# Skip factors loaded as one row, and the compressed keys and values computed in two column halves of the array, in a decoder trunk block on one core

## The chip, the cores and the metric

The kernel runs on one core of one Trainium2 chip, as a single launch. The metric is the device time of a run in microseconds, as the median of several runs. The profile is of one execution, and its span is a little shorter than that execution's time.

## What is computed

One layer of a decoder trunk on `x` of shape (1, 512, 1024), fp32: 512 tokens (S), width 1024 (D).

```
h = RMSNorm(x);  u = h @ W_in            # one projection, its columns split among the heads below
y_A = DSA(u_A) @ W_br_A                  # an index picks 128 keys a query, then softmax attention
y_B = NSA(u_B) @ W_br_B                  # compressed keys, selected blocks, window; gated sum
y_C = SSD(u_C) @ W_br_C                  # Mamba-2: causal conv, chunked scan, gated RMSNorm
x = x + (sig(g_A) y_A + sig(g_B) y_B + sig(g_C) y_C) @ W_out
x = x + relu(RMSNorm(x) @ W_1)^2 @ W_2
```

Two small parts of it matter here:

```
# NSA: 31 blocks of 32 tokens, 16 apart, become one compressed key and one compressed value each
blocks = a[:, win_idx] + pos                       # a = keys (v = 0) or values (v = 1), 2 head groups
k_cmp  = rms_norm(einsum('bnlgd,lde->bnge', blocks, w[0]), gain);  v_cmp = einsum(..., w[1])
# SSD: a skip term with one factor for each of the 32 heads
y = y_diag + y_off + xs * d_skip
```

## The kernel before, in words

All big matrices are multiplied in three float32r products: both operands are split into a high part (a rounding copy, on ScalarE) and a low part (the difference, on VectorE or GpSimd), and high x high, high x low and low x high are summed in PSUM (`mm3`, lines 458 to 460). Weights come in blocks of 128 x 1024 by a stream (`WS`): a load on SP's queue into one of three raw buffers (line 154), a split into `whi` (line 173) and `wlo` (line 175) in one of six buffers each. The next load into a raw buffer waits until its split is done, and the next split until a block has been used up.

At the start the input is loaded in four blocks of 128 tokens (t = 0 to 3) and normalised; PE transposes each block in two halves (line 427) into PSUM tiles `pT`, of which there are two, and ScalarE and VectorE write the transposed block as `hTh` (line 437) and `hTl` (line 438). A `pT` tile is free again when both have read it. Beside it runs the first projection, `c0` (DSA's key and value, the index's operands, dt), token block after token block: 24 matmuls of 456 columns for each.

Two generators are interleaved in program order by estimated PE time. The filler makes the projections, in the order c0, nkv, dq, z, x, nq and then the gates and the branch products. The main one makes the DSA index with its top-k steps on VectorE (lines 899 and 900), DSA's attention, the SSD scan and NSA's attention. Which instruction follows which on an engine is then set by the scheduler of the Tile framework, which has a time model of its own and some written-out priorities; on each engine the instructions run in that order.

Small constants (gains, convolution weights, dt's bias and so on) are loaded in `const_load`, called in the filler when block t = 1 of c0 is done, all on SP's queue. Some come as rows and are transposed on PE in `const_cols`, called at block t = 1 of nkv, and copied from PSUM by VectorE (lines 355 to 359). The skip factors are wanted as `dcol`, 128 partitions x 16, one column for each 128 channels, with one head in partitions 0 to 63 and another in 64 to 127, halved. The scaling of the convolved channels in `conv` (line 860) reads it.

In `cmp_prep` the compressed keys and values are made on PE, for each of the two in 16 fp32 matmuls, one for each pair of positions of a block (line 659). The stationary operand is `xc`, 128 x 64 (two positions x 64 dims by 2 groups x 32 blocks), the streamed one 64 columns of the weights. An fp32 matmul shows as two passes in the trace, with a weight load each.

Of the kernel before, what the change touches and what calls it, by code (L numbers as in the profile page):

```python
# [9 lines left out]
AF = mybir.ActivationFunctionType  # L10
ALU = mybir.AluOpType
# [30 lines left out]
def build_kernel(ctx, tc, A, out):  # L42
    nc = tc.nc
    pe, act, dve, pool = nc.tensor, nc.scalar, nc.vector, nc.gpsimd
    done = set()

    def dram(ap, off, dims):
        return bass.AP(tensor=ap.tensor, offset=ap.offset + off, ap=dims)

    def bc(ap, shape):  # L50
        return ap.to_broadcast(shape)

    def f(ap):
        return ap.bitcast(F32)
# [37 lines left out]
    def ps(tag, shape, dt=F32, bufs=2):  # L92
        if tag == XT[0]:
            XT[1] += 1
            if XT[1] % 3 == 0:
                tag = "pF"
        return psp.tile(shape, dt, tag=tag, name=tag, bufs=PSB[tag])
# [27 lines left out]
    p = ps("pF", [128, 512])  # L125
# [159 lines left out]
    for q in range(3):  # L285
        m = 0
# [32 lines left out]
    dcol = cp.tile([128, 16], F32, name="dcol")  # L319
    CL = {}  # L320

    def const_load():
        def put(t, ap, n, rows=None):
            nc.sync.dma_start(t, dram(ap, 0, [[n, rows] if rows else [0, 128], [1, n]]))

        def rows(name, ap, r, n=128):
            CL[name] = early.tile([r, n], F32, name=name)
            put(CL[name], ap, n, r)

        def wide(name, ap, n):  # L330
            CL[name] = early.tile([128, n], F32, name=name)
            put(CL[name], ap, n)
        wide("gq_d", A["dsa_q_norm"], 64)
        wide("gk_d", A["dsa_k_norm"], 64)
        wide("gq_n", A["nsa_q_norm"], 64)
        wide("gk_n", A["nsa_k_norm"], 192)
        rows("rows1", A["ssd_conv_w"], 96)
        rows("rows2", A["ssd_conv_b"], 24)
        rows("rows3", A["ssd_norm_g"], 16)
        rows("posr", A["nsa_cmp_pos"], 64, 64)  # L340
        put(dtb, A["ssd_dt_bias"], 32)
        put(alog, A["ssd_a_log"], 32)
        for e in range(2):
            nc.sync.dma_start(dcol[64 * e:64 * e + 64], dram(A["ssd_d"], e, [[0, 64], [2, 16]]))
        dve.tensor_scalar(dcol, dcol, 0.5, None, op0=ALU.mult)
        dve.tensor_tensor(g_dsa, CL["gq_d"], CL["gk_d"], op=ALU.mult)
        dve.tensor_tensor(g_nsa, CL["gk_n"].rearrange("p (a b) -> p a b", b=64), bc(CL["gq_n"][:, None, :], [128, 3, 64]), op=ALU.mult)

    def const_cols():
        p = ps("pT", [128, 512])  # L350
        pe.transpose(p[:, 0:96], CL["rows1"], ident[:96, :96])
        pe.transpose(p[:, 96:120], CL["rows2"], ident[:24, :24])
        pe.transpose(p[:64, 120:184], CL["posr"], ident[:64, :64])
        pe.transpose(p[:, 184:200], CL["rows3"], ident[:16, :16])
        dve.tensor_copy(convc, p[:, 0:120])
        dve.tensor_copy(gcol, p[:, 184:200])
        pv_ = p[:64, 120:184].rearrange("p (v a l) -> p v a l", v=2, l=2)
        dve.tensor_copy(pos2[0:64], pv_[:, :, :, 0])
        dve.tensor_copy(pos2[64:128], pv_[:, :, :, 1])
# [29 lines left out]
    for t in range(NB):  # L389
        with tc.high_priority(offset=0 if t else HP):  # L390
# [5 lines left out]
            else:  # L396
# [3 lines left out]
                for k0 in range(0, KT, 4):  # L400
                    p = ps("pT", [128, 4, 128])
# [11 lines left out]
            else:  # L413
# [4 lines left out]
                for c in (0, 512):  # L418
                    p = ps("sc", [128, 512])
# [3 lines left out]
            for k0 in range(0, KT, 4):  # L423
                if t:
                    p = ps("pT", [128, 4, 128])
# [19 lines left out]
    for i, b in enumerate((2, 3)):  # L445
        for half in range(2):
            cur = 2 * b + half
            r = slice(64 * half, 64 * half + 64)
# [82 lines left out]
    def rms_rows(pl, src, rows, nb, scale, bias):  # L531
        sqt = pl.tile([128, NB, 64], F32, name="sqk")
        dve.tensor_tensor(sqt[:rows, :nb], src, src, op=ALU.mult)
        st = pl.tile([128, NB], F32, name="stk", bufs=2)
        dve.tensor_reduce(st[:rows, :nb], sqt[:rows, :nb], AX.X, ALU.add)
        dve.tensor_scalar(st[:rows, :nb], st[:rows, :nb], scale, bias, op0=ALU.mult, op1=ALU.add)
        rt = pl.tile([128, NB], F32, name="rtk", bufs=2)
        pool.tensor_tensor(rt[:rows, :nb], st[:rows, :nb], mhalf[:rows, :nb], op=ALU.pow)
        return rt
# [96 lines left out]
    def cmp_prep(u1, e1):  # L636

        for v in range(2):
            xc = e1.tile([128, 16, 2, 32], F32, name="xc", bufs=1)
            wh = []  # L640
            for i in range(2):
                w_ = e1.tile([128, 8, 64], F32, name="cmpw", tag="cw", bufs=2)
                nc.sync.dma_start(w_, dram(A["nsa_cmp_w"], v * 131072 + i * 65536, [[64, 128], [8192, 8], [1, 64]]))
                wh.append(w_)
            pool.memset(xc[:, :, :, 31:32], 0.0)
            p = ps("pT", [128, S])
            for t in range(NB):
                pe.transpose(p[:, t * 128:t * 128 + 128], u1[:, t, v * 128:v * 128 + 128], ident)
            yield 440
            for g in range(2):  # L650
                for half in range(2):
                    r = slice(64 * half, 64 * half + 64)
                    base = p[64 * g:64 * g + 64, half:half + 1]
                    win = bass.AP(tensor=base.tensor, offset=base.offset, ap=[base.ap[0], [2, 16], [16, 31]])
                    dve.tensor_tensor(xc[r, :, g, :31], win, bc(pos2[r, v, :, None], [64, 16, 31]), op=ALU.add)
            yield 440
            pc = ps("pT", [128, 512])
            for a in range(16):
                pe.matmul(pc[:64, :64], xc[:, a].rearrange("p g n -> p (g n)"), wh[a // 8][:, a % 8], start=a == 0, stop=a == 15)
            if v == 0:  # L660
                kx = e1.tile([64, 64], F32, name="kx")
                dve.tensor_copy(kx, pc[:64, :64])
                yield 1800
                rt = rms_rows(e1, kx[:, None, :], 64, 1, 1.0 / 64, EPS)
                dve.scalar_tensor_tensor(kx, kx, rt[:64, 0:1], g_nsa[:64, 0, :], op0=ALU.mult, op1=ALU.mult)
                kcs = e1.tile([64, 2, 2, 64], F32R, name="kcs")
                kxb = bc(kx[:, None, :], [64, 2, 64])
                act.activation(kcs[:, 0], kxb, AF.Copy)
                dve.tensor_tensor(kcs[:, 1], kxb, f(kcs[:, 0]), op=ALU.subtract)
                for i in range(2):  # L670
                    pk = ps("pT", [128, 64], F32R)
                    pe.transpose(pk, kcs[:, i].rearrange("p a b -> p (a b)"), identr[:64, :64])
                    act.activation(kc[:, :, i], f(pk).rearrange("p (g n) -> p g n", g=2), AF.Copy)
                yield 600
            else:
                vx = e1.tile([64, 64], F32, name="vx")
                dve.tensor_copy(vx, pc[:64, :64])
                yield 1800
                sel = e1.tile([64, 2, 4, 32], F32, name="sel")
                dve.tensor_copy(sel, bc(ident[:64, 0:64].rearrange("p (g n) -> p g n", g=2)[:, :, None, :], [64, 2, 4, 32]))  # L680
                zero = e1.tile([128, 256], F32, name="zero")
                pool.memset(zero, 0.0)
                vzf = vz.rearrange("p a b c d -> p (a b c d)")
                for z in range(2):
                    act.activation(vzf[:, 256 * z:256 * z + 256], zero, AF.Copy)
                for g in range(2):
                    pk = ps("pT", [128, 64])
                    pe.matmul(pk, sel[:, g].rearrange("p a b -> p (a b)"), vx, start=True, stop=True)
                    for h in range(4):
                        r = slice(32 * h, 32 * h + 32)  # L690
                        act.activation(vz[r, g, h % 2, 0], pk[r], AF.Copy)
                        dve.tensor_tensor(vz[r, g, h % 2, 1], pk[r], f(vz[r, g, h % 2, 0]), op=ALU.subtract)
                    yield 300

    def filler():
# [40 lines left out]
        def do_nkv():  # L736
# [27 lines left out]
            def rest():  # L764
                for g in range(2):
                    tr = make_k(u2[:, :, 64 * g:64 * g + 64], g_nsa[:, 2, :], K[f"w{g}"])
                    yield 0
                    tr()
                    yield 0
                dve.tensor_scalar(gate, gate, 0.5, 0.5, op0=ALU.mult, op1=ALU.add)  # L770
                yield from cmp_prep(u1, e1)
                pclose("e1")
                pclose("early")
                done.add("nkv")
# [1030 lines left out]
    while True:  # L1805
        with tc.high_priority(offset=HI[0]):
            r = next(mg, None)
# [42 lines left out]
```

## Time and profile before

| What | us |
|---|---|
| median of 3 runs | 1374.2 (1374.09 to 1375.94) |
| the profiled execution: time, span | 1373.8, 1372.1 |
| PE busy | 1334.8 |
| VectorE (DVE) busy | 995.5 |
| ScalarE (ACT) busy | 727.6 |
| GpSimd (POOL) busy | 269.9 |

Lines of the profile name an engine, a line of the kernel and a tile: `PE pT L427` is the matmul of line 427 that writes `pT`. PEld is PE's weight load, SPq, ACTq and so on are the queues of an engine, and a load is named by its destination and source. An idle time is shown with what released it.

### The profile page before, as it was taken

Reading aid. Unit: us, or ns where it says so; the run is one execution under the profiler, and the core shown is the slowest. Engines: PE = TensorE matmul, PEld = TensorE weight load, DVE = VectorE, ACT = ScalarE, POOL = GpSimd, SP = SyncE. Lnnn points to the kernel's source line nnn. Section 1 sums busy time; section 2 is a strip of 40 time slices with the busy share of each in tenths; the row PEclk is TensorE's granted clock in tenths of the full one; section 3 lists DMA queues with packets and bytes.
Section 4 is the critical chain, followed back from the end, with each engine's and each line's share of the span. In section 5 each row is a group of like instructions: output and inputs, shape, how many; then the busy total and the mean of one; then the engine's idle time right before and its main releaser. Section 6 shows DMA issues by size and latency. Waiting matters only on the chain.

```text
span 1372.1 us, 19609 instructions
## 1 busy us (share of the span) xinstructions
PE 1334.8 (97%) x6827; PEld 1113.0 (81%) x6827; DVE 995.5 (73%) x1970; ACT 727.6 (53%) x1393; POOL 269.9 (20%) x242
## 2 busy tenths in 40 slices
PE   6899999999999999999999999999999999999998
PEld 5788888888887777888888888787879888888887
DVE  4469997788987767457768798979745666767741
ACT  4355525577777776347666655656334344444430
POOL 2135201111005667600000021113001201102000
PEclk8899999999999999999999999999999999999999
DMA  4335655555559999564336453434535655746531
GB/s 141 99 116 144 163 161 150 152 135 155 143 145 327 304 276 318 181 176 119 112 113 180 119 152 117 147 119 144 193 94 168 129 165 125 182 114 130 151 123 50
DMA packets 253713, 213.73 MB, mean 156 GB/s; under 512 B 17817, under 2 KB 205101, under 8 KB 253614
## 3 DMA queue, kind: packets, MB, share of 16 engines
q1 hardware_dynamic: 237644, 188.88, 45.9%
q0 software_dynamic: 15232, 20.98, 8.1%
q10 hardware_dynamic: 738, 2.63, 0.5%
q8 instruction: 54, 0.88, 0.3%
q14 instruction: 45, 0.37, 0.1%
HBM read 171.74 MB, written 40.70 MB: 155 GB/s over the span
## 4 chain that ended last, share of the span: by engine, by line
PE 82%; DMA 7%; DVE 6%; ACT 2%; issue 2%; POOL 1%; SPq 0%; DVEq 0%; ACTq 0%; POOLq 0%
PE pj L458 19%; PE pj L459 19%; PE pj L460 19%; PE sc L460 3%; PE sc L459 3%; PE sc L458 3%; PE pT L983 2%; DMA dcol<-in_ssd_d_dram 2%; PE sc L924 2%; PE sc L923 2%; PE pv L995 2%; PE pv L996 1%; PE sc L1311 1%; DMA yr<-yc_d 1%; DMA E<-ac_d 1%
## 5 line engine op out<-in xcount | busy, mean ns | idle before, releaser
L173 ACT ACTIVATE whi<-wraw 128x1024 fp32r<-128x1024 f32 (+2 forms) x190 | 198.3, 1047 | 256.9 <-PE pj L459 136.8
L175 DVE TENSOR_TENSOR wlo<-wraw,whi 128x1024 fp32r<-128x1024 f32 (+1 forms) x176 | 223.3, 1273 | 99.6 <-ACT whi L173 99.2
L458 PE MATMUL pj<-hTh,whi 128*128 128x512 f32 x512 | 203.7, 398 | 2.3 <-DVE cacc L852 2.0
L460 PE MATMUL pj<-hTh,wlo 128*128 128x512 f32 x512 | 202.6, 396 | 0.0
L459 PE MATMUL pj<-hTl,whi 128*128 128x512 f32 x512 | 202.4, 395 | 0.0
L932 ACT ACTIVATE p<-p,nb,rs 128x256 f32<-128x256 f32 (+3 forms) x160 | 107.8, 676 | 34.2 <-DVE nb L930 34.1
L458 PEld LDWEIGHTS pj<-hTh,whi 128*128 128x128 f32 x512 | 96.7, 189 | 21.8 <-ACT eab L1340 2.2
L460 PEld LDWEIGHTS pj<-hTh,wlo 128*128 128x128 f32 x512 | 96.7, 189 | 18.9 <-issue 0.2
L459 PEld LDWEIGHTS pj<-hTl,whi 128*128 128x128 f32 x512 | 96.5, 189 | 18.5 <-issue 0.2
L458 PE MATMUL pj<-yh,whi 128*128 128x512 f32 (+1 forms) x288 | 106.1, 373 | 4.1 <-ACT yh L828 3.1
L459 PE MATMUL pj<-yl,whi 128*128 128x512 f32 (+1 forms) x288 | 107.2, 372 | 0.1
L460 PE MATMUL pj<-yh,wlo 128*128 128x512 f32 (+1 forms) x288 | 106.1, 368 | 0.0
L459 PE MATMUL pj<-h2l,whi 128*128 128x512 f32 (+1 forms) x256 | 96.3, 376 | 0.0
L460 PE MATMUL pj<-h2h,wlo 128*128 128x512 f32 (+1 forms) x256 | 96.2, 376 | 0.0
L458 PE MATMUL pj<-h2h,whi 128*128 128x512 f32 (+1 forms) x256 | 96.1, 376 | 0.0
L458 PE MATMUL pj<-whi,hTh 128*128 128x512 f32 (+2 forms) x208 | 81.4, 391 | 3.2 <-DVE v_s L560 2.2
L460 PE MATMUL pj<-whi,hTl 128*128 128x512 f32 (+2 forms) x208 | 80.6, 388 | 0.0
L459 PE MATMUL pj<-wlo,hTh 128*128 128x512 f32 (+2 forms) x208 | 80.1, 385 | 0.0
L1042 POOL DMA_DIRECT2D qu<-q_d x32 | 23.6, 738 | 272.4 <-PE sc L924 165.5
L987 ACT ACTIVATE pth<-pT 128x512 fp32r<-128x512 f32 x95 | 54.9, 593 | 32.1 <-PE pT L983 28.6
L458 PE MATMUL sc<-whi,fh 128*128 128x512 f32 x168 | 65.4, 389 | 0.0
L459 PE MATMUL sc<-wlo,fh 128*128 128x512 f32 x168 | 65.4, 389 | 0.0
(408 smaller groups left out, 3159.5 us busy)
## 6 DMA issues: line engine op xcount, KB each, us to landing
wraw<-in_w_in_dram SPq DMA_DIRECT2D x84, 512.0 KB, 3.9
wraw<-in_w_ff_dram SPq DMA_DIRECT2D x58, 512.0 KB, 4.1
qd<-in_w_ff_dram POOLq DMA_DIRECT2D x18, 512.0 KB, 5.8
gld<-g_d SPq DMA_DIRECT2D x35, 256.0 KB, 2.7
q_d<-qev SPq DMA_DIRECT2D x64, 128.0 KB, 3.3
qu<-q_d POOLq DMA_DIRECT2D x32, 256.0 KB, 3.6
E<-ac_d SPq DMA_DIRECT2D x16, 512.0 KB, 6.7
xz<-xzt_d SPq DMA_DIRECT2D x16, 512.0 KB, 5.2
```

The lines of the kernel that those rows point to most:

```text
L173: act.activation(hi[:, :m], r[:, :m], AF.Copy)
L175: (pool if i in LOWP else dve).tensor_tensor(lo[:, :m], r[:, :m], f(hi[:, :m]), op=ALU.subtract)
L458: pe.matmul(o, lh, rh, start=first, stop=False)
L459: pe.matmul(o, lh, rl, start=False, stop=False)
L460: pe.matmul(o, ll, rh, start=False, stop=last)
L923: pe.matmul(s_[:, h % w, :n], u.q[h], kh[:, :n], start=True, stop=False)
L924: pe.matmul(s_[:, h % w, :n], u.q[h], kl[:, :n], start=False, stop=True)
L932: act.activation(u.p[h][:, :n], u.p[h][:, :n], AF.Exp, bias=u.nb[:, h:h + 1], scale=rs8[:, u.b, u.h0 + h:u.h0 + h + 1], accum_out=u.sm[:, ...
L983: pe.transpose(pt[:, h], u.p[h][:, kb * 128:kb * 128 + 128], ident)
L987: act.activation(ph, ptf, AF.Copy)
L995: pe.matmul(o, vk, ph0, start=st, stop=False)
L1042: pool.dma_start(q.rearrange("p (i a) c -> p i (a c)", i=2), src)
```

## The change

The skip factors are no longer loaded into `dcol` by two loads of single numbers from the 32 factors. One load brings all 32 as a row, the same for all 128 partitions, into a tile `dsk` (`wide` is the helper for that, used for other constants too). Two VectorE instructions in `const_cols`, one for each half of the partitions, then write every second factor, halved, to `dcol`. The one VectorE instruction that halved `dcol` in `const_load` goes.

The 16 products of `cmp_prep` alternate between the lower 64 and the upper 64 PSUM partitions of the output, that is, between two column halves of the array. So each half has 8 of the 16 positions summed up. ScalarE copies the upper half to SBUF, and VectorE adds the lower half to it, where VectorE copied the one sum before.

```diff
@@ const_load
         put(dtb, A["ssd_dt_bias"], 32)
         put(alog, A["ssd_a_log"], 32)
-        for e in range(2):
-            nc.sync.dma_start(dcol[64 * e:64 * e + 64], dram(A["ssd_d"], e, [[0, 64], [2, 16]]))
-        dve.tensor_scalar(dcol, dcol, 0.5, None, op0=ALU.mult)
+        wide("dsk", A["ssd_d"], 32)
@@ const_cols
         dve.tensor_copy(convc, p[:, 0:120])
         dve.tensor_copy(gcol, p[:, 184:200])
+        for e in range(2):
+            r = slice(64 * e, 64 * e + 64)
+            dve.tensor_scalar(dcol[r], CL["dsk"].rearrange("p (m e) -> p m e", e=2)[r, :, e], 0.5, None, op0=ALU.mult)
@@ cmp_prep
             for a in range(16):
-                pe.matmul(pc[:64, :64], xc[:, a].rearrange("p g n -> p (g n)"), wh[a // 8][:, a % 8], start=a == 0, stop=a == 15)
+                o_ = 64 * (a % 2)
+                pe.matmul(pc[o_:o_ + 64, :64], xc[:, a].rearrange("p g n -> p (g n)"), wh[a // 8][:, a % 8], start=a < 2, stop=a > 13)
             if v == 0:
                 kx = e1.tile([64, 64], F32, name="kx")
-                dve.tensor_copy(kx, pc[:64, :64])
+                act.activation(kx, pc[64:128, :64], AF.Copy)
+                dve.tensor_tensor(kx, kx, pc[:64, :64], op=ALU.add)
...
                 vx = e1.tile([64, 64], F32, name="vx")
-                dve.tensor_copy(vx, pc[:64, :64])
+                act.activation(vx, pc[64:128, :64], AF.Copy)
+                dve.tensor_tensor(vx, vx, pc[:64, :64], op=ALU.add)
```

## The prediction

> **What bounds the kernel now.** I read the page first: the busy shares, then the chain that ended last.
>
> ```profile
> span 1372.1 us, 19609 instructions
> PE 1334.8 (97%) x6827; PEld 1113.0 (81%) x6827; DVE 995.5 (73%) x1970; ACT 727.6 (53%) x1393; POOL 269.9 (20%) x242
> PE pj L458 19%; PE pj L459 19%; PE pj L460 19%; PE sc L460 3%; PE sc L459 3%; PE sc L458 3%; PE pT L983 2%; DMA dcol<-in_ssd_d_dram 2%; PE sc L924 2%; PE sc L923 2%; PE pv L995 2%; PE pv L996 1%; PE sc L1311 1%; DMA yr<-yc_d 1%; DMA E<-ac_d 1%
> ```
>
> PE is the bound: it is idle in only 1372.1 - 1334.8 = 37.3 us, so a gain must shorten PE's work or fill an idle stretch. The odd item of the chain is a load: dcol, which holds 16 numbers a partition. Next, the waits of the first 60 us (total, times, longest).
>
> ```profile
> ACT hTh L437 <- PE pT L427: 25.7, 4, 16.6
> DVE dcol L345 <- DMA dcol<-in_ssd_d_dram: 18.0, 1, 18.0
> PE pT L427 <- DVE hTl L438: 15.4, 1, 15.4
> ```
>
> So VectorE stands 18.0 us at the halving of dcol, and PE has one wait of 15.4 us, 41% of all its idle time. The chain of the same window (start, us, what) shows how they hang together.
>
> ```profile
> 17.60 22.15 DMA dcol<-in_ssd_d_dram
> ...
> 39.85 0.17 DVE dcol L345
> 40.02 0.60 DVE hTl L438
> ...
> 40.67 1.12 PE pT L427 x4
> 41.79 0.38 PE sc L460
> ...
> 45.97 0.38 PE sc L459
> 46.35 0.70 PE pT L427 x4
> 47.05 0.21 PE sc L460
> ...
> 53.87 0.21 PE sc L460
> 54.08 0.23 PE pj L458
> ```
>
> The second load lands at 39.75; L345 runs; the hTl subtraction queued behind it frees a pT bank; PE can then transpose token block 3. PE restarts slowly: its 12 matmuls from 41.79 to 46.35 take 0.38 us each, the 34 from 47.05 to 54.08 take 7.03 / 34 = 0.207. At 54.08 the first projection (c0) is over and nkv begins. The timeline says what was ready meanwhile.
>
> ```profile
> 20.79 1.10 DVE L175 TENSOR_TENSOR wlo<-wraw,whi 128x912 fp32r<-128x912 f32 x1
> 22.36 1.08 ACT L437 ACTIVATE hTh<-pT 128x512 fp32r<-128x512 f32 x2 [2.77 <-PE pT L427]
> 23.34 1.06 ACT L173 ACTIVATE whi<-wraw 128x1024 fp32r<-128x1024 f32 x1
> 24.89 0.36 PE L459 MATMUL sc<-wlo,hTh 128*128 128x456 f32 x1
> 39.93 1.28 DVE L438 TENSOR_TENSOR hTl<-pT,hTh 128x512 fp32r<-128x512 f32 x2
> ```
>
> VectorE's last work ends at 21.89, both hTh halves are there at 23.44, and the two hTl subtractions need 1.28: without the wait they end near 24.7, before PE runs dry at 24.89 + 0.36 = 25.25.
>
> **The change, part by part.** First the loads: KB each and median us to landing; then an issue on SP.
>
> ```profile
> dcol<-in_ssd_d_dram SPq DMA_DIRECT2D x2, 4.0 KB, 12.4
> alog<-in_ssd_a_log_dram SPq DMA_DIRECT2D x1, 16.0 KB, 2.9
> wraw<-in_w_in_dram SPq DMA_DIRECT2D x84, 512.0 KB, 3.9
> 21.92 7.21 SPq L154 DMA_DIRECT2D wraw<-in_w_in_dram  x1
> ```
>
> Two loads of 64 x 16 single numbers, every second one, become one load of a contiguous row of 32 on 128 partitions. That is exactly the shape of alog, issued just ahead of dcol, which landed in 2.9 us with four times the bytes. The small loads also held SP: the weight load issued at 21.92 took 7.21 us to issue. I take 2.9 us for the new load. It stays at its place in SP's queue, as one issue instead of two, for which I count nothing.
>
> The halving leaves VectorE's early queue and goes, as two instructions, behind the copies of the column constants. There, and in the work after it, the trace has:
>
> ```profile
> 79.27 0.18 DVE L359 COPY pos<-pT 64x32 f32<-64x32 f32 x1
> 79.48 1.92 DVE L894 SCALAR_TENSOR_TENSOR mask<-irelu,iwt,caus 128x256 f32<-128x256 f32 x1
> 81.91 2.60 DVE L533 TENSOR_TENSOR sqk<-u 128x256 f32<-128x256 f32 x1
> 85.69 0.41 PE pj L458
> ```
>
> The load is long there by then. But VectorE is late at this place: the chain runs through sqk to PE at 85.69, so two instructions like L359's, 2 x 0.17, can push PE back. I count +0.3; the lower end is 0 (PE's wait there has other causes beside), the upper 0.4. The first reader of dcol, the scaling in conv (L860), comes at 290 us.
>
> The stall goes whole, by this working. PE's way from 25.25 to 54.08 is 28.83 us. Unstalled it is 2 x 0.70 for the transposes, 12 x 0.207 and the 7.03 of the rest: 1.40 + 2.48 + 7.03 = 10.91. The gain is 28.83 - 10.91 = 17.92: 15.42 idle, 0.42 on the first transposes and 2.08 of slow matmuls. What is late next? nkv would begin near 36.2. Its first weight block was split on ScalarE at 23.34, and the next two, issued by 21.92, need 3.9 us once nothing blocks them: there by about 26. The fourth is issued when VectorE has split the first (near 26) and lands near 30; nkv uses blocks 0 and 1 for two token blocks first, 4 x 6 x 0.23 = 5.5 us, so wants it at 41. So the cover is over 10 us. Everything after hangs on PE and moves forward with it.
>
> The products of the compressed keys and values: the chain's rows for the 16 fp32 matmuls (32 passes) of each, with the row after, and those of a product already written to alternating column halves (sc<-E,xt) and a full-width one beside it.
>
> ```profile
> 125.91 2.01 PE pT L659 x32
> 127.92 0.43 PE pj L460
> ...
> 155.80 2.01 PE pT L659 x32
> ...
> 469.86 0.89 PE sc L1311 x8
> ...
> 471.61 1.03 PE sc L1311 x16
> ```
>
> A pass of L659 takes 2.01 / 32 = 63 ns with 64 columns streamed. The full-width L1311 takes 0.89 / 8 = 111 ns for 128 columns, and the alternating one 1.03 / 16 = 64 ns, also for 128. So alternating halves do run side by side, but a pass comes no faster than 63 to 64 ns, whether 64 or 128 columns wide. L659 is at that floor already. I take no gain; the ends are -2.0 (both products halved) and +0.4, since the matmul behind L659 takes 0.43 instead of 0.23 and that 0.2 could come once more for each product. The Trainium skill, "TensorEngine Tiling (Array Packing)", section Theoretical Speedup, gives a factor up to 2 where a free dimension is at most 64; by that the products would take 2.0 us less. Its page "TensorE: Matmul & The Clock Gate" (Wait — 56ns, not 53.3ns?) knows an issue cost of about 62 ns per matmul with hardware decode off, by which nothing is gained; L659's 63 ns agrees. "Key Properties" of the tiling page speaks against the change, as changing the mode drains the engine; L659's 0.43 may be such a cost, already paid.
>
> Reading the result out: instead of one VectorE copy from PSUM, ScalarE copies the upper half and VectorE adds.
>
> ```profile
> L662 DVE COPY kx<-pT x1: 205/205/205, 128.9 to 128.9; 64x64 f32<-64x64 f32 x1
> L692 DVE TENSOR_TENSOR vz<-pT,vz x8: 194/220/231, 165.2 to 169.5; 32x64 fp32r<-32x64 f32 x8
> L673 ACT ACTIVATE kc<-pT x2: 224/224/224, 142.3 to 143.6; 128x64 fp32r<-128x64 f32 x2
> 128.61 0.60 ACT L893 ACTIVATE irelu<-sc 128x512 f32<-128x512 f32 x1 [1.42 <-PE sc L891]
> ACT whi L173 <- issue: 8.1, 3, 4.4
> ```
>
> VectorE's part is equal within 0.02 us. ScalarE's 0.22 fits for kx: it idles 1.42 us before 128.61, while the products end at 127.92 and VectorE comes at 128.9. The added wait is VectorE's on that copy; behind it stand the top-k steps of the index, which set the masks. If ScalarE is held by a weight split waiting for its buffer, VectorE waits too: at most 4.4 us, the longest of ScalarE's such waits in 100 to 180 us, for each product. The nearest rows say zero for kx; I take +0.2 for both, ends 0 and 8.8.
>
> Sum: -17.9 + 0.3 + 0 + 0.2 = -17.4. The profiled execution took 1373.8, its span and 1.7 around; 1373.8 - 17.4 = 1356.4. The median of the runs shown is 0.4 above it: **1356.8 us**.
>
> **The rivals.**
> The halves do overlap, against the floor I read: 2.0 less, 1354.8. For it speaks the 64 ns of a twice as wide pass; against it that the narrow one is no faster.
>
> PE's slow restart stays, or a weight block comes late by as much: only the idle 15.4 is won, so 1373.8 - 15.4 + 0.5 + 0.4 = 1359.3. For it: PE has just done transposes when it comes there; against it: the matmuls ahead of them ran at 0.21.
>
> ScalarE's copy holds VectorE, the rival on the other side: 8.8 at most by the row above, minus the 0.2 counted, gives 1365.4. It decides against the change only if VectorE waits over 17.4 us more in the two places and all of it reaches PE; the transposes that need kx follow 13 us after it, and no wait of ScalarE in that window comes near half of it.
>
> The change doesn't do what it says: the new load is as slow, or another load in the same stretch holds VectorE as long: 1374.2. alog's 2.9 us speaks against it.
>
> Last, a scheduler with a time model orders every engine's queue, so an edit can reorder work far from it. From PE's later waits (the largest group is 3.1 us in three) I estimate up to 5 us either way, 1352 to 1362 around the forecast.
>
> ```profile
> PE pj L458 <- ACT yh L828: 3.1, 3, 1.2
> ```
>
> **How the numbers follow.** Forecast 0.60, halves overlap 0.14, slow restart or late block 0.10, copy holds VectorE 0.06 (0.02 of it past break-even), no effect 0.03, reordering past its 5 us in the good or bad direction 0.07. The range holds the first three with the reordering, 0.84 less what falls off its edges: 1352 to 1363. About 0.2% is what a measurement of this kernel can tell from no change. Faster by more: all but 0.02 past break-even and 0.03 without effect, 0.95; within: 0.03; slower: 0.02.
>
> **What would show it.** Right: no wait of VectorE for a load of ssd_d, no PE idle of microseconds between 20 and 40 us, matmuls of the last two token blocks of c0 at 0.21 throughout, nkv's first matmul near 36, and the products still near 2.0 us each. Wrong in part: the products near 1.0; 0.38 us matmuls after 25; VectorE idle on kx or vx. The forecast as a whole fails if another wait for a load stands in VectorE's queue before 40 us, or if PE waits for nkv's weights near 36.

## The result, and the profile after

| | median, us | lowest to highest |
|---|---|---|
| before | 1374.2 | 1372.68 to 1375.94 |
| changed | 1364.12 | 1362.66 to 1369.46 |

The ratio is 0.9936, with an interval of 0.9910 to 0.9961. The change makes the kernel faster by 10.1 us, where 17.4 were forecast. The five runs of the changed kernel lie in two groups, three near 1363 and two near 1369; the profile is of the slowest, so it is read here for places and not for its end.

The span and the busy times of the profile after:

```profile
span 1367.7 us, 19598 instructions
PE 1335.8 (98%) x6827; PEld 1110.2 (81%) x6827; DVE 993.2 (73%) x1971; ACT 729.4 (53%) x1395; POOL 277.8 (20%) x242
```

PE's idle time fell from 37.3 to 1367.7 - 1335.8 = 31.9 us only, although a wait of 15.4 was to go. Did that wait go? The timeline around the old stall, VectorE first, then PE (start, us, engine, line, operation):

```profile
20.73 0.35 DVE L357 TENSOR_SCALAR dcol<-dsk 64x16 f32<-64x16 f32 x2 [0.18 <-DMA dsk<-in_ssd_d_dram]
21.79 1.29 DVE L439 TENSOR_TENSOR hTl<-pT,hTh 128x512 fp32r<-128x512 f32 x2 [0.70 <-ACT hTh L438]
...
23.66 0.37 PE L460 MATMUL sc<-wlo,hTh 128*128 128x456 f32 x1
23.86 0.60 PE L428 MATMUL pT<-ident,x 128*128 128x128 f32 x4
24.22 0.45 PE L461 MATMUL sc<-whi,hTl 128*128 128x456 f32 x1
...
34.05 0.37 PE L461 MATMUL sc<-whi,hTl 128*128 128x456 f32 x1
34.26 0.39 PE L459 MATMUL pj<-whi,hTh 128*128 128x512 f32 x1
```

It did. VectorE waits 0.18 us for the row instead of 18.0 for the single numbers, the transposes (L428) follow the matmuls with no gap, and nkv begins at 34.26 where it began at 54.08: PE is 19.8 us ahead at this place. At the end the medians show 10.1: about half of the lead is given back. So the question is where, and by which part of the change.

### The profile page after: what moved, and what is told of

The parts are those of the page before. It is cut to its first block, busy times and chain, and to the rows that moved or that the text cites. A ratio compares the mean times of both kernels' runs of the same rounds, so it can differ in the third digit from the quotient of the medians.

```text
span 1367.7 us, 19598 instructions
## 1 busy us (share of the span) xinstructions
PE 1335.8 (98%) x6827; PEld 1110.2 (81%) x6827; DVE 993.2 (73%) x1971; ACT 729.4 (53%) x1395; POOL 277.8 (20%) x242
## 5 line engine op out<-in xcount | busy, mean ns | idle before, releaser
L936 ACT ACTIVATE p<-p,nb,rs 128x256 f32<-128x256 f32 (+3 forms) x160 | 107.8, 676 | 40.2 <-DVE nb L934 38.3
L459 PEld LDWEIGHTS pj<-yh,whi 128*128 128x128 f32 x288 | 53.9, 190 | 19.4 <-ACT yh L832 7.6
L992 DVE TENSOR_TENSOR ptl<-pT,pth 128x512 fp32r<-128x512 f32 x95 | 64.0, 680 | 3.2 <-ACT pth L991 3.0
```

Of the source, the lines that this page charges most:

```text
L459: pe.matmul(o, lh, rh, start=first, stop=False)
L936: act.activation(u.p[h][:, :n], u.p[h][:, :n], AF.Exp, bias=u.nb[:, h:h + 1], scale=rs8[:, u.b, u.h0 + h:u.h0 + h + 1], accum_out=u.sm[:, ...
L992: dve.tensor_tensor(pl, ptf, f(ph), op=ALU.subtract)
```

## The experiments

One comparison stands ahead of them, of instructions and not of times. The row load alone leaves the order of the instructions as before, but for dcol's own load and halving: PE's 6,827 weight loads stand in the same sequence in the traces of before and e1. As soon as the read-out of the products is edited, the scheduler puts more than a quarter of them at other places, far from the edit. Call these the old order (before) and the new order (after). Two theories follow. Theory 1: the stall is worth what was forecast, and the edit of products and read-out costs some 8 us, by the order that it brings. Theory 2, the rival: the work that starts earlier collides later with transfers and buffers, so the stall was worth only some 8 us, and the rest is neutral.

**The two parts alone, the products without the halves, and the change again.** The edits, in this sequence:

```
e1_row_only            the diff of const_load and const_cols alone
e2_halves_only         the diff of cmp_prep alone; the two loads of single numbers stay
e3_row_sum_order       e1, products in one half as before, and for kx (vx alike), instead of the copy:
                       +  act.activation(kx, pc[:64, :64], AF.Copy)
                       +  dve.tensor_tensor(kx, kx, pc[:64, :64], op=ALU.max)
e4_changed_again       the changed kernel
```

> The skip factors' row load alone; the products of the compressed keys and values as before. The scheduler's order of every engine is then that of the kernel before, but for the halving of dcol and its load. Theory 1 (the order costs): the changed kernel was 19.7 us ahead at nkv and lost about 10 us of it to the other order that the products' edit brings; here nothing reorders, so the lead stays: 1374.2 - 19.6 = about 1354.6 us. Theory 2 (the earlier front collides later with transfers and buffers, whatever the order): the lead is given back here too, and the products' 1.9 us is missing: about 1366 us.

> The column halves and their sum alone; the skip factors loaded by single numbers as before, so the 15.4 us stall of PE stays. Its order is that of the changed kernel on PE. Theory 1 (the order costs): 1374.2 - 1.9 + about 11 = 1383 us, slower than before. Theory 2 (the earlier front collides later): no earlier front, so only the products' gain: 1372.3 us.

> Row load, products in one half as before, but read out by ScalarE's copy and a VectorE instruction (a maximum of the copy and the same sum, which leaves the value as it is). The scheduler's PE order is within 31 lines of that of the changed kernel and 1,477 lines from that of the kernel before. Theory 1: the order's cost is there without column halves: 1364.1 + 1.9 = about 1366 us, and 11 us over the row load alone. Theory 2: about 1366 us as well, but the row load alone is at 1366 too. A third view, that the column halves themselves slow PE down (a drain at the switch of the tiling): then this kernel has no such cost and lies near 1355 us.

> The changed kernel again, the same in every queue, with the lines numbered as before, on the same chip as the three others: 1364 us, with runs near 1363 and near 1369 as shown before. It gives the interval of the changed kernel beside the others, and a second profile to see which waits differ between its two groups of runs.

| | median, us | ratio to before (1374.94) | order |
|---|---|---|---|
| e1, row load alone | 1357.05 | 0.9870 [0.9853, 0.9888] | old |
| e2, halves alone | 1383.14 | 1.0061 [1.0047, 1.0075] | new |
| e3, row load and two-step read-out | 1362.92 | 0.9915 [0.9901, 0.9930] | new |
| e4, the change | 1364.27 | 0.9930 [0.9912, 0.9948] | new |

Theory 2 falls: the row load alone gives 1374.94 - 1357.05 = 17.9 us, and the other part alone costs 1383.14 - 1374.94 = 8.2. e3 shows that the column halves themselves are not the cost, since it has none and stands with e4. What e2, e3 and e4 share is the read-out in two steps and the new order (the same sequence on PE in e2, e4 and after, and all but the same in e3).

**The order by itself.** Each engine's queue is held to a given order by edges between its instructions, without waits on semaphores: the changed kernel in the old order (but for ScalarE's two new copies and the two new halvings, which the scheduler places), and the row-load kernel, with no instruction other than e1's, in the new one. In the traces PE's sequence is then that of before in e5 and that of after in e6.

```
for each engine:                       # e5: kernel changed, old order; e6: kernel e1, new order
    for prev, nxt in consecutive(order[engine]):
        tc.add_manual_dep(nxt, prev.name, NoSync)
```

> The changed kernel with every engine's queue written out by hand in the order of the kernel before (ordering edges only, no waits; ScalarE's two new copies and the two new halvings are placed by the scheduler). Theory 1 (the other order costs the 7 us between the row load alone and the changed kernel): as the row load alone, less the 1.9 us that the trace shows for the two products: 1357.1 - 1.9 = 1355.2 us. Rival (the column halves or their sum cost time wherever they stand, by a drain or by VectorE's wait on ScalarE): 1362 to 1364 us.

> The row load alone, products as before, with every engine's queue written out in the order of the changed kernel; no instruction differs from the row load alone. Theory 1 (the order costs): 1364.3 + 1.9 = about 1366 us. Rival (the halves and their sum cost, not the order): 1357 us, as the row load alone.

| | order | median, us | ratio |
|---|---|---|---|
| e1, row load | old | 1357.05 | 0.9870 [0.9853, 0.9888] |
| e6, row load | new | 1367.4 | 0.9949 [0.9930, 0.9967] |
| e5, changed | old | 1356.73 | 0.9870 [0.9855, 0.9885] |
| e4, changed | new | 1364.27 | 0.9930 [0.9912, 0.9948] |

The same instructions cost 10.3 us more in the new order (e6 against e1) and 7.5 more (e4 against e5). In the old order the changed kernel takes what e1 takes. So the order is the cost, and not the halves or the read-out; e5, which has the edges too, shows no cost of the edges. The size is less sure than the fact: e3, with nearly the new order, no halves and no edges, stands only 1362.92 - 1357.05 = 5.9 us above e1, and each of these medians has an interval of some 2 us to both sides. Where the cost is paid shows in PE's windows (us, busy, granted clock, DMA share, GB/s), first of e1, then of e6:

```profile
300.00:500.00 200.00, 194.44 (x1082) 0.99 0.74 228
700.00:960.00 260.00, 253.72 (x1350) 1.00 0.47 140
```

```profile
300.00:500.00 200.00, 197.85 (x1092) 0.99 0.72 223
700.00:960.00 260.00, 245.04 (x1269) 1.00 0.45 128
```

From 700 to 960 PE does 8.7 us less in e6, and from 300 to 500 3.4 us more. The clock is the same. Over the whole spans PE is idle 1363.0 - 1333.8 = 29.2 us in e6 and 1355.0 - 1332.0 = 23.0 in e1, so idle time accounts for 6.2 of the 8.0 us between these two profiles. The 260 us hold the product of the SSD branch with W_br_C, with NSA's attention between its matmuls. From the first to the last of the 16 splits of that product's operand (L828, L832 after) the windows of PE are, for e1, e6 and the changed kernel's profile:

```profile
762.50:854.60 92.10, 88.67 (x444) 1.00 0.48 138
```

```profile
753.00:861.90 108.90, 100.19 (x495) 1.00 0.43 123
```

```profile
755.50:866.10 110.60, 101.08 (x488) 0.97 0.42 121
```

In the new order this stage begins 9.5 us earlier, with more attention matmuls in it, and ends 7.3 us later. PE is idle 3.4 us of it in e1, 8.7 in e6 and 9.5 in the profile after, whose clock was also a little lower there (0.97). The waits of PE between 700 and 960 us (total, times, longest), for the same three:

```profile
PE pj L458 <- ACT yh L828: 3.3, 3, 1.4
PE pv L1151 <- DVE yt L1013: 1.6, 1, 1.6
```

```profile
PE pj L458 <- ACT yh L828: 4.9, 5, 1.6
PE pj L459 <- DVE yl L829: 2.3, 3, 0.9
PE pj L458 <- ACT yh L831: 2.1, 2, 1.4
PE pv L996 <- DVE ptl L988: 1.9, 2, 1.3
```

```profile
PE pj L459 <- ACT yh L832: 5.7, 4, 2.2
PE pj L460 <- DVE yl L833: 2.7, 3, 1.1
PE pv L1000 <- DVE ptl L992: 1.7, 1, 1.7
```

No single wait carries the idle time. It is many waits of 1 to 2 us for operands that ScalarE and VectorE split (yh, yl) or write (ptl) just ahead of PE.

**Which part of the stall was VectorE's, and which the blocked weight queue.** With the slow loads left in place, the halving alone is put behind the copies of the column constants. Then, in a second kernel, the slow loads go to ScalarE's queue as well.

```
e7   const_load:  the two loads stay;  -  dve.tensor_scalar(dcol, dcol, 0.5, ...)
     const_cols:  +  with tc.issue_after(gcol_copy): dve.tensor_scalar(dcol, dcol, 0.5, ...)
e9   e7, and  -  nc.sync.dma_start(dcol[...], ...)    +  act.dma_start(dcol[...], ...)
```

> The kernel before with its two slow loads of dcol, but the halving, and so VectorE's wait for them, queued behind the copies of the column constants (at 79 us before); the order is otherwise that of the kernel before. If VectorE's wait was all of the stall, the time is that of the row load alone, 1357 us. If the weights queued behind the slow loads come late too (nothing moved on the DMA engines from 20 to 30 us, and a weight load took 7.2 us to issue), PE runs out of weights at the start of nkv, near 35 us, and waits until they land at about 40 and are split: 6 us and up to 2 us of slow restart, so 1363 to 1366 us.

> As the kernel with VectorE's wait moved, but the two slow loads of dcol are issued on ScalarE's queue, where the scheduler places them near 7 us; 12 of PE's 5,831 rows in the order differ. If the weights were late because they stood behind the slow loads in SP's queue, they now pass them and land in about 4 us: 1357 to 1358 us, as the row load alone. If the slow loads hold the DMA engines themselves, the weight loads issued between 7 and 30 us are late whatever their queue: PE waits 5 us and more before 45 us, and the time is 1363 us or above.

e7 took 1366.99 us (0.9941 [0.9927, 0.9955]), 9.9 more than e1, and e9 1374.84 (1.0001 [0.9991, 1.0011]). In e7 VectorE no longer waits for dcol, and PE runs dry later, at 35 us, for another reason: v_d stands in VectorE's queue behind the low part of a weight block, and that behind ScalarE's split of the block. PE's longest wait; ScalarE's split; and the window 20 to 30 us (busy times of PE, PEld, DVE, ACT, POOL, then clock, DMA share, GB/s):

```profile
PE pT L595 <- DVE v_d L560: 8.2, 1, 8.2
```

```profile
40.55 1.06 ACT L173 ACTIVATE whi<-wraw 128x1024 fp32r<-128x1024 f32 x1 [12.25 <-DMA wraw<-in_w_in_dram]
```

```profile
20.00:30.00 10.00, 10.00 (x58) 9.11 (x57) 4.76 (x8) 4.04 (x11) 0.00 (x0) 1.00 0.05 0
```

The weights queued behind the two slow loads move nothing for these 10 us and are split at 40.55. So to take away VectorE's wait alone wins about half of the 17.9 us (1374.97 - 1366.99 = 8), and late weights keep the other 10; only the row takes away both. The two overlap in time, and no run takes away the late weights alone. On ScalarE's queue (e9) the slow loads do no better, but they also run earlier there, issued near 4 us beside the loads of the input, so this isn't the same collision. e9's rows for the next input block and the next weight block on ScalarE, and a wait of SP's queue:

```profile
17.22 1.06 ACT L393 ACTIVATE sq_junk<-x 128x1024 bf16<-128x1024 f32 x1 [7.75 <-DMA x<-in_x_dram]
28.74 0.96 ACT L173 ACTIVATE whi<-wraw 128x912 fp32r<-128x912 f32 x1 [9.85 <-DMA wraw<-in_w_in_dram]
...
SPq L305 <- DMA dcol<-in_ssd_d_dram: 6.8, 1, 6.8
```

The loads on SP's own queue come late while the small ones run on ScalarE's, and PE waits for weights from 14 us on:

```profile
PE pj L458 <- ACT whi L173: 15.7, 1, 15.7
```

**Other orders of the same instructions.** What in the new order costs? Theory 1a was that DSA's or NSA's attention lags behind the projections, and so its results come just ahead of the branch products. A number in the source sets how much projection work goes between the steps of the attention, as a ratio of estimated PE times:

```
-R0, R1, R2, R3 = 1000.0, 1.5, 2.5, 0.5
+R0, R1, R2, R3 = 1000.0, 1.4, 2.5, 0.5      # e8; 1.35 in e10, 1.45 in e11, 1.6 in e12
```

> The changed kernel with one number changed, the ratio that interleaves DSA's attention with the projections (1.4 for 1.5): the attention's and the scan's PE rows then stand 8 to 30 places later than in the order before, where those of the changed kernel stand 11 to 60 later. Theory 1a (the other order costs because the attention and the scan fall behind the projections, so that the branch products and the attention's end meet with VectorE and ScalarE full): half or more of the 7 us come back, 1358 to 1361 us. Rival 1b (it is the detail of the order, and not that lag): it stays at 1364 us or moves either way.

> The changed kernel with the interleaving ratio at 1.35: PE's attention rows stand 11 to 50 places later than in the order before, and at the end of the attention still 16 to 54 later. If a lag of the attention behind the projections is what costs, this is as slow as the changed kernel or slower, 1363 us or above. If the time hangs on details of the order, anywhere between 1355 and 1368 us.

> The changed kernel with the ratio at 1.45: the attention's rows stand 11 to 38 places later than in the order before in its first half and 21 to 87 places earlier at its end. If the lag costs, this lies near the order before, 1355 to 1358 us. If the time hangs on details of the order, anywhere between 1355 and 1368 us.

> The changed kernel with the ratio at 1.6: the attention's rows stand 11 to 44 places later in the first half and within 11 places of the order before at the end. If the lag costs, between the ratio of 1.4 and the changed kernel, 1358 to 1362 us. If the time hangs on details of the order, anywhere between 1355 and 1368 us.

The last columns are of the profiles: when the last split (L828) of the SSD branch's stage starts, how long the stage takes from the first split, and PE's idle time in it. The granted clock was 1.00 there in all six.

| R1 | median, us | ratio | last split at | stage, us | idle, us |
|---|---|---|---|---|---|
| 1.35 (e10) | 1355.3 | 0.9861 [0.9843, 0.9878] | 847.6 | 95.4 | 2.7 |
| 1.4 (e8) | 1358.11 | 0.9879 [0.9862, 0.9895] | 855.5 | 95.3 | 1.5 |
| 1.45 (e11) | 1359.99 | 0.9896 [0.9881, 0.9910] | 860.4 | 99.2 | 3.3 |
| 1.5 (the change, e4) | 1364.27 | 0.9930 [0.9912, 0.9948] | 859.9 | 107.8 | 7.6 |
| 1.6 (e12) | 1355.41 | 0.9859 [0.9843, 0.9876] | 849.8 | 94.9 | 2.8 |
| 1.5, old order (e5) | 1356.73 | 0.9870 [0.9855, 0.9885] | 852.7 | 91.9 | 3.2 |

Six orders of one set of instructions lie between 1355.3 and 1364.3 us. 1.5 is the worst of them. The time rises with the ratio up to 1.5 and is low again at 1.6: e10 and e12, on opposite sides, agree within 0.2 us. Theory 1a falls with e10, in which the attention's rows still stand 16 to 54 places later at its end (by the expectation) and which is the fastest. What the five faster orders have is a shorter stage of the SSD branch, 92 to 99 us against 108, with less idle time. The same window, first to last split, for e10:

```profile
752.20:847.60 95.40, 92.69 (x469) 1.00 0.48 137
```

It begins as early as in e6 and still loses only 2.7 us. The feature of the order that decides stays open, and so does which engine's order it is, since e5 and e6 hold all of them at once. Shown is that the order costs, and in which stage PE stands idle for it. That idle time is only a part: between the profiles of e4 and e5 PE's idle time differs by 28.5 - 24.0 = 4.5 us and its busy time by 1333.6 - 1329.2 = 4.4, and why PE is busy longer with the same instructions is not shown.

## Why the prediction was wrong, step by step

**The stall: right, the last digit by luck.** Forecast 17.92, measured 17.9 by the row load alone (e1), where PE's wait is gone and nkv begins here:

```profile
34.62 0.39 PE L458 MATMUL pj<-whi,hTh 128*128 128x512 f32 x1
```

That is 54.08 - 34.62 = 19.5 us earlier, more than the forecast. At the end of the two profiles 1372.1 - 1355.0 = 17.1 of it are left; their matmuls stand in the same sequence, and their starts, compared one by one, show that some 2 us are lost again between 400 and 1000 us, for which the working had no term. The slow restart did not stay: after the transposes the matmuls follow each other at 0.21 us. The row landed in 4.3 us instead of 2.9, which cost VectorE 0.18. That the slow loads also held SP was named but given no price; with VectorE's wait moved away it still costs about 10 us (e7).

**The halving: right in size, wrong in place.** The step put it at 79 us and counted 0.3. The scheduler put it at 20.73, ahead of L439, where its 0.35 us lie beside PE's work.

**The products: wrong.** The step read 63 to 64 ns a pass as a floor and took no gain. Its row of 64 ns was of alternating passes of 128 columns, against 111 ns at full width, so it showed the overlap and not a floor; that it came near the 63 ns of a single narrow pass was chance. The row of before, the rows after, and the window of the line alone after:

```profile
125.84 2.08 PE L659 MATMUL pT<-cmpw,xc 128*64 128x64 f32 x32
```

```profile
107.71 1.15 PE L661 MATMUL pT<-cmpw,xc 128*64 128x64 f32 x32
108.79 0.50 PE L461 MATMUL pj<-whi,hTl 128*128 128x512 f32 x1
```

```profile
107.00:110.00 3.00, 1.15 (x32) 1.01 (x32) 1.00 0.85 245
```

1.15 / 32 = 36 ns a pass, against 2.08 / 32 = 65 before: 0.93 less for each of the two, 1.86 together, within the end of -2.0 that was kept. The matmul behind takes 0.50 as it did before, so the 0.2 kept for that didn't come. Halves do run side by side for 64 columns too, and the 62 ns a matmul that the prediction cites bound nothing here. The Trainium skill's "TensorEngine Tiling (Array Packing)", section Theoretical Speedup, had a factor up to 2; the trace agrees with 2.08 / 1.15 = 1.8. The rival "halves overlap" had the mechanism, but not the time. Whether the 1.86 us reach the end is not settled: the medians of e5 and e1 differ by 0.3 us and those of e4 and e6, in the new order, by 3.1, with intervals that allow 1.86 in both. The profiles of e5 and e1 show what can become of it, since their matmuls have the same sequence. At 150 us e5 is 2.2 ahead, 1.9 of it from the products. Then it has a wait that e1 has not, and slow matmuls behind it:

```profile
152.52 0.50 PE L458 MATMUL pj<-hTh,whi 128*128 128x512 f32 x1 [1.83 <-DVE zo L732]
...
153.60 0.63 PE L458 MATMUL pj<-hTh,whi 128*128 128x512 f32 x1
```

zo is read out by VectorE, which is busy there, with top-k steps among others. PE came earlier and waited for it, and its granted clock was 0.62 from 152 to 156 us. At 160 e5 is 1.1 behind; by the end it is 1.8 ahead again, from other places.

**The read-out: right.** ScalarE's copy and VectorE's sum for kx:

```profile
L664 ACT ACTIVATE kx<-pT x1: 222/222/222, 109.0 to 109.0; 64x64 f32<-64x64 f32 x1
L665 DVE TENSOR_TENSOR kx<-kx,pT x1: 193/193/193, 110.3 to 110.3; 64x64 f32<-64x64 f32 x1
```

The copy ends at 109.2, and VectorE comes 1.1 us later and does not wait for it. For vx the copy ends at 138.6 and VectorE comes at 139.3. The rival in which it waits up to 8.8 us would have given 1365.4, near the result, by a mechanism that is not there: the time alone would have named the wrong cause.

**The step that failed** is the last rival: the reordering "up to 5 us either way", set symmetrically about the forecast, so that it stands in the sum at nothing. It is the term that was mis-sized. It measured +7.5 (e4 against e5) and +10.3 (e6 against e1), or +5.9 by e3, and the largest wait of the profile before, 3.1 us in three, was no bound for it: as far as PE is idle, the loss is the sum over many such waits. The forecast of 1356.8 is what the change takes in the old order (1356.73). So near an agreement is partly luck, since the lead at nkv was larger than forecast and some of it was lost again.

## What to carry to other kernels

Where a scheduler sets the order of the queues, compare the order before and after an edit first; if it moved, the edit's own price is measured with the order held, and the order is a cost of its own, here 0.55 to 0.75% of the time. A few neighbouring values of a parameter that shifts the interleaving are worth running for the same reason: 1.35 or 1.6 in place of 1.5 brings the changed kernel to 1355.3 and 1355.4 us, the lowest medians here, though their intervals overlap that of the old order (e5). Constants that are read as every second single number are better loaded as a row and picked apart on an engine: loads queued behind the single numbers came some 10 us late, and a wait moved away from them (e7) wins only half.

## What the hardware showed beside that

Two loads of 64 x 16 single numbers, 4 KB each, took 22 us together in the profile before, and next to nothing moved meanwhile: a DMA share of 0.05 and 0 GB/s between 20 and 30 us in e7. In e9 they ran on ScalarE's queue, and SP's loads of other data were late all the same, the input block 17.22 - 9.78 = 7.4 us later on ScalarE than in e7 (whose row stands at 9.78). So in that run the slow loads held up more than the queue that issued them. After its wait of 1.83 us PE ran at a granted clock of 0.62 for about 4 us in e5, with 0.43 us from matmul to matmul in place of 0.23. And a 64-column fp32 pass took 36 ns in alternating halves, where the prediction had read 63 as the least that a pass can take.
